# Column and row halves by turns in the chunk loop, the merge and the A products of a hybrid decoder block

## The chip, the cores and the metric

The kernel runs on one core of a Trainium2 chip. The metric is the device time of one execution in microseconds; the median of three runs is given. The engines are named as in the profile: PE (TensorE), with its weight loads as PEld, DVE (VectorE), ACT (ScalarE), POOL (GpSimd) and SP (SyncE, which issues the DMAs).

## The reference

A decoder block for a sequence of 2,048 tokens and a width of 1,024: RMS norm and modulation, one input projection, a convolution branch, an RWKV-7 branch with 16 heads of 64, gates, output projections, residual, final norm. The change touches the recurrence of the RWKV-7 branch:

```python
def step(state, inp):
    r_t, w_t, k_t, v_t, kk_t, b_t = inp
    sk = jnp.einsum('bhvk,bhk->bhv', state, kk_t)
    state = (state * w_t[:, :, None, :] - sk[..., None] * b_t[:, :, None, :]
             + v_t[..., None] * k_t[:, :, None, :])
    return state, jnp.einsum('bhvk,bhk->bhv', state, r_t)
```

## The kernel before

The sequence is cut into 4 blocks of 512 tokens, the 16 heads into 8 pairs of two heads (`hh` = 0, 1; each head has 64 of the 128 partitions), and two pairs (`q` = 0, 1) make a group: 4 groups a block, 16 in all. In a group the recurrence runs over 8 chunks of 64 tokens (`NCH` = 8, `CH` = 64): 128 chunks in all. Even and odd chunks (`e` = 0, 1) keep their rows in opposite halves of the partitions: `prow(e)` holds the rows of the solution, `vrow(e)` those of the values.

What a pair and a group do, in order:

- `pair` projects k, r and v (`mm3`, L195: an input of 128x512 against 128x128 weights in three products of high and low parts, recorded as passes with 256 or 512 columns), builds `KR` and `BK`, and the *A products* (L525): for each chunk and head one product of `BK` and `KR`, masked and evacuated to `As` by DVE (L527). So that one head's product can use all 128 partitions, ACT copies `BK` into `BKz`, whose other head's partitions are zero (L518). Four chunks of one head fill one PSUM bank (`aux`, two banks, which other steps of `pair` share).
- The inverse of a 64x64 triangle per chunk and head is made of its two 32x32 diagonal blocks, which POOL inverts (L594, L596; a DMA through DRAM before and behind it), and of the *merge*, which makes the off-diagonal block with 32x32 matmuls: L626 (lower), a DVE copy to `Qs` (L630), L635 (upper), a DVE copy into `As` (L640). Even and odd chunks are two runs of 16 matmuls each, first all of e = 0, then all of e = 1, in one PSUM bank (`late`).
- The *chunk loop* (L657 to L697). For each chunk: the state against `KR` (L668), the values against `As` (L673, 64 rows), DVE copies the sum to `X` (L676), the o matmuls of the chunk before (`olast`, L653) and their copy by ACT (L655), the *solution* (L682: `As` against `X`, 64 rows), DVE scales it into `uv` (L684), the state's update (L688) and four DVE operations that write the state `S` (L693). The next chunk begins with that state. Each of L653, L673 and L682 has four matmuls with 64 columns a chunk. Each chunk takes a new PSUM tile `xo` of two.

All f32 matmuls are issued as two passes, each with a weight load; the profile counts passes. The f32r ones of L195 are one pass each.

A scheduler orders the instructions of each engine by its own estimate of times and by priorities, so projections of the next pair, the convolution and the gates (`fill`) stand between the steps of the chunk loop in PE's queue, and DVE's 30 convolution taps a tile (L759) between the steps on DVE. Each engine works through its queue in order. `tc.issue_after(x)` keeps an instruction behind x in that order. L493 (`pair`) sums squares per chunk with 64-column matmuls whose output goes to the two partition halves by turns. Phase 2 (from L904 on: output projections, norm) is not touched.

Of the kernel before, what the change touches and what calls it, by code (L numbers as in the profile page):

```python
# [82 lines left out]
def hybrid_block(ctx: ExitStack, tc: tile.TileContext, x, vecs, convk, w2a2, final_g, ada, w_in, w_co, w_ro, w_o, crow, out,  # L83
# [193 lines left out]
    BKz = c1.tile([P, 2, NCH // 2, 4 * CH], F32, name="BKz")  # L277
    nc.gpsimd.memset(BKz[64:128, 0], 0.0)
    nc.gpsimd.memset(BKz[0:64, 1], 0.0)
    hones = bones.bitcast(F32)[:, 0::64]  # L280
    one = c1.tile([P, CH], F32, name="one")
# [164 lines left out]
    def pair(b, q_, pr, h, lora, uv, Asb, rn, res):  # L446
# [69 lines left out]
        for hh in range(2):  # L516
            hs = slice(64 * hh, 64 * hh + 64)
            nc.scalar.copy(BKz[hs, hh], BK[hs])  # L518
        for c4 in range(NCH // 4):
            for hh in range(2):  # L520
                pA = pa.tile([P, 2, 256], F32, name="aux", tag="aux")
                for c in range(4):
                    cc, e = (c4 * 4 + c) // 2, c % 2
                    es = slice(e * 128, e * 128 + 128)
                    nc.tensor.matmul(pA[:, c // 2, es], BKz[:, hh, cc, es], KR[:, cc, es],  # L525
                                     start=(c == 0), stop=(c == 3), skip_group_check=True)
                nc.vector.tensor_tensor(  # L527
                    out=Asb[:, hh, c4 * 4:c4 * 4 + 4, :].rearrange("p (a e) n -> p a (e n)", e=2),
                    in0=pA, in1=flat(maskA).unsqueeze(1).broadcast_to([P, 2, 256]), op=ALU.mult)
# [31 lines left out]
    def group(b, g, h, lora, fill):  # L561
        uv = l3.tile([P, NCH, 2, P], F32, name="uv", tag="uv", bufs=2)
        As = [l3.tile([P, 2, NCH, P], F32, name="As", tag="As", bufs=ASB) for _ in range(2)]
# [53 lines left out]
        pq = pl.tile([P, 2, 2, NCH // 2, 32], F32, name="late", tag="late")  # L617
        for e in range(2):
# [4 lines left out]
        for e in range(2):  # L623
            lo_, hi_ = quarters(e)
            for n, (q, hh, c) in enumerate(every):
                nc.tensor.matmul(pq[hi_, q, hh, c, :], As[q][lo_, hh, 2 * c + e, hi_], T11[lo_, q, hh, c, :],  # L626
                                 start=(n == 0), stop=(n == 15), skip_group_check=True)
        for e in range(2):
            lo_, hi_ = quarters(e)
            nc.vector.tensor_copy(Qs[hi_], pq[hi_])  # L630

        for e in range(2):
            lo_, hi_ = quarters(e)
            for n, (q, hh, c) in enumerate(every):
                nc.tensor.matmul(pq[lo_, q, hh, c, :], Qs[hi_, q, hh, c, :], As[q][hi_, hh, 2 * c + e, hi_],  # L635
                                 start=(n == 0), stop=(n == 15), skip_group_check=True)
        for e in range(2):
            lo_, hi_ = quarters(e)
            for q in range(2):
                nc.vector.tensor_copy(As[q][lo_, :, e::2, hi_], pq[lo_, q])  # L640
# [4 lines left out]
        prev = None  # L645

        def olast(c, xo):

            vr, rc = vrow(c % 2), rcol(c % 2)
            for q in range(2):  # L650
                for hh in range(2):
                    hs = slice(64 * hh, 64 * hh + 64)
                    nc.tensor.matmul(xo[vr, q, hs], As[q][:, hh, c, rc], uv[:, c, q, hs],  # L653
                                     start=False, stop=(q == 1 and hh == 1), skip_group_check=True)
            nc.scalar.copy(O[vr, c // 2], xo[vr, 0:2])  # L655

        for c in range(NCH):  # L657
            cc, e = c // 2, c % 2
            pr_, vr = prow(e), vrow(e)
# [467 lines left out]
```

## Time and profile before

| | |
|---|---|
| median of 3 runs | 3123.53 us (3115.43 to 3130.16) |
| the profiled execution | 3119.74 us, of which the span of the trace is 3118.0 us |
| granted clock of TensorE, mean | 0.984 |
| A products L525 | 1024 passes, 136.6 us busy |
| o L653, values L673, solution L682 | 1024 passes each; 87.3, 87.2 and 89.7 us busy |
| merge L626 and L635 | 1024 passes each; 36.0 and 33.9 us busy |
| projections L195 with 256 columns | 3 × 4608 passes, 958 us busy each |
| convolution taps L759 on DVE | 928, 698.0 us busy |
| DMA | 667.79 MB, mean 214 GB/s |

Passes are pipelined and overlap in the trace, so their busy times add up to more than PE's share of the span; what a pass costs is read from the distance between starts. A row of a group reads: line, engine, operation, output<-inputs, tile of the array, shape, count, then busy time and mean ns of one, then the engine's idle time before them and what ended it. A row of a timeline reads: start, duration, engine, line, operation and count of what was merged.

### The profile page before, as it was taken

How to read it: one execution, taken by the hardware profiler on the slowest of the kernel's cores; microseconds unless marked ns; L12 is line 12 of the kernel's file. 1: busy time of each engine (PE TensorE's matmuls, PEld its weight loads, DVE VectorE, ACT ScalarE, POOL GpSimd, SP SyncE). 2: the span in 40 equal slices, each digit the busy share in tenths (PEclk: the TensorE clock that was granted, in tenths of full speed). 3: DMA queues.
4: the chain of work that ended last, by engine and by line, in shares of the span. 5: the costliest groups of instructions: out<-in, count | busy, mean ns of one | idle time of the engine just before them, and what ended most of it. 6: DMA issues, size and time to landing. Idle time of an engine off the chain costs nothing. (4 is left out here: it accounts for less than half of the span.)

```text
span 3118.0 us, 64926 instructions
## 1 busy us (share of the span) xinstructions
PE 2980.5 (96%) x25648; PEld 2804.4 (90%) x25648; DVE 2138.2 (69%) x4282; ACT 1018.6 (33%) x1868; POOL 1142.4 (37%) x1708
## 2 busy tenths in 40 slices
PE   6799998999999999999999999999999999799998
PEld 6689998989999999999999999999999978678888
DVE  6676867686767676767676677767688535986633
ACT  4424343433233332323232414132332213342311
POOL 3354435433433325142424335316256013653100
PEclk9899999999999999999999999999999999899999
DMA  7665758573747476547565767646458657777665
GB/s 297 214 239 193 258 187 278 192 236 133 251 139 256 136 242 230 197 138 233 159 221 166 260 211 262 196 142 208 139 178 267 215 204 271 282 250 274 216 223 176
DMA packets 354849, 667.79 MB, mean 214 GB/s; under 512 B 134704, under 2 KB 153456, under 8 KB 354544
## 3 DMA queue, kind: packets, MB, share of 16 engines
q1 hardware_dynamic: 354544, 663.64, 63.2%
q8 instruction: 202, 3.31, 0.4%
q14 instruction: 103, 0.84, 0.1%
HBM read 483.07 MB, written 179.31 MB: 212 GB/s over the span
## 5 line engine op out<-in xcount | busy, mean ns | idle before, releaser
L195 PE MATMUL ps_main<-h_hi,w_hi 128*128 128x256 f32 x4608 | 958.1, 285 | 24.4 <-ACT w_hi L178 19.1
L195 PE MATMUL ps_main<-h_hi,w_lo 128*128 128x256 f32 x4608 | 958.6, 285 | 9.0 <-POOL w_lo L180 7.6
L195 PE MATMUL ps_main<-h_lo,w_hi 128*128 128x256 f32 x4608 | 958.1, 285 | 0.0
L195 PEld LDWEIGHTS ps_main<-h_hi,w_hi 128*128 128x128 f32 x4608 | 718.3, 189 | 35.9 <-ACT w_hi L178 20.2
L195 PEld LDWEIGHTS ps_main<-h_hi,w_lo 128*128 128x128 f32 x4608 | 716.7, 189 | 18.0 <-POOL w_lo L180 9.4
L195 PEld LDWEIGHTS ps_main<-h_lo,w_hi 128*128 128x128 f32 x4608 | 716.3, 189 | 7.3 <-issue 0.7
L759 DVE SCALAR_TENSOR_TENSOR acc<-u,ck,acc 128x512 f32<-128x512 f32 x928 | 698.0, 752 | 20.1
L594 POOL TENSOR_TENSOR itmp<-La,TT 128x126 f32<-128x126 f32 (+22 forms) x496 | 179.4, 362 | 147.5 <-DMA La<-dA 112.0
L693 DVE SCALAR_TENSOR_TENSOR S<-xo,pe,Se 64x64 f32<-64x64 f32 x512 | 144.9, 283 | 107.9 <-PE xo L688 98.6
L178 ACT CAST w_hi<-w_st 128x1024 fp32r<-128x1024 f32 x103 | 107.9, 1048 | 293.7 <-DMA w_st<-w_in_t 144.0
L596 POOL TENSOR_TENSOR TT<-TT,itmp 128x126 f32<-128x126 f32 (+22 forms) x496 | 190.0, 383 | 35.8
L663 ACT ACTIVATE Se<-S,pe 128x128 f32<-128x128 f32 x256 | 88.9, 394 | 228.7 <-DVE S L693 228.3
L180 POOL TENSOR_TENSOR w_lo<-w_st,w_hi 128x1024 fp32r<-128x1024 f32 x47 | 112.2, 2388 | 136.8 <-ACT w_hi L178 98.2
L548 POOL TENSOR_TENSOR vv<-rk,vv 128x512 f32<-128x512 f32 x32 | 43.5, 1359 | 295.7 <-ACT rk L547 295.7
L684 DVE TENSOR_TENSOR uv<-xo,rn 64x256 f32<-64x256 f32 x128 | 53.8, 421 | 131.8 <-PE xo L682 130.7
L525 PE MATMUL aux<-KR,BKz 128*128 128x128 f32 x1024 | 136.6, 278 | 2.6 <-DVE As L527 1.8
L180 DVE TENSOR_TENSOR w_lo<-w_st,w_hi 128x1024 fp32r<-128x1024 f32 x56 | 75.6, 1349 | 82.4 <-PE ps_main L195 51.3
L525 PEld LDWEIGHTS aux<-KR,BKz 128*128 128x128 f32 x1024 | 123.8, 191 | 5.0 <-DVE As L527 2.0
L527 DVE TENSOR_TENSOR As<-aux,maskA 128x512 f32<-128x512 f32 x128 | 86.9, 687 | 46.7 <-PE aux L525 46.1
L676 DVE COPY X<-xo 64x256 f32<-64x256 f32 x128 | 53.7, 420 | 91.6 <-PE xo L673 90.7
L655 ACT COPY uv<-xo 64x256 f32<-64x256 f32 x128 | 46.8, 366 | 186.2 <-PE xo L653 185.7
L668 PE MATMUL xo<-S,KR 128*128 128x128 f32 x512 | 95.7, 279 | 1.2 <-DVE S L693 1.1
(290 smaller groups left out, 5497.5 us busy)
## 6 DMA issues: line engine op xcount, KB each, us to landing
w_hi<-kh_in SPq DMA_DIRECT2D x219, 512.0 KB, 3.9
w_lo<-kl_in SPq DMA_DIRECT2D x219, 512.0 KB, 5.0
w_st<-w_in_t SPq DMA_DIRECT2D x73, 512.0 KB, 4.6
kh_in<-w_hi SPq DMA_DIRECT2D x71, 512.0 KB, 3.0
kl_in<-w_lo SPq DMA_DIRECT2D x71, 512.0 KB, 4.5
w_hi<-kh_ro SPq DMA_DIRECT2D x32, 512.0 KB, 4.3
w_lo<-kl_ro SPq DMA_DIRECT2D x32, 512.0 KB, 5.8
w_st<-w_co_t SPq DMA_DIRECT2D x32, 512.0 KB, 3.5
```

What stands on the lines that cost most here:

```text
L178: nc.scalar.copy(hi, st)
L180: lo_eng.tensor_tensor(out=lo, in0=st, in1=hi.bitcast(F32), op=ALU.subtract)
L195: nc.tensor.matmul(ps[:, qs], ww[:, k, :], aa[k][:, qs], start=(k == 0 and t == 0 and q == 0), stop=(k == KT - 1 and t == 2 and q == ms - ...
L525: nc.tensor.matmul(pA[:, c // 2, es], BKz[:, hh, cc, es], KR[:, cc, es], start=(c == 0), stop=(c == 3), skip_group_check=True)
L527: nc.vector.tensor_tensor(out=Asb[:, hh, c4 * 4:c4 * 4 + 4, :].rearrange("p (a e) n -> p a (e n)", e=2), in0=pA, in1=flat(maskA).unsqueeze ...
L594: nc.gpsimd.tensor_tensor(out=tmp[:, :ni, :nt], in0=La[:, j:j + 1, j + 1:].broadcast_to([P, ni, nt]), in1=TT[:, :ni, j:j + 1].broadcast_to ...
L596: nc.gpsimd.tensor_tensor(out=TT[:, :ni, j + 1:], in0=TT[:, :ni, j + 1:], in1=tmp[:, :ni, :nt], op=ALU.add)
L663: nc.scalar.mul(Se[:, q, :], Sg[:, q, :], R[q]["pe"][:, c:c + 1])
L668: nc.tensor.matmul(xo[:, q, :], R[q]["KR"][:, cc, es], Sg[:, q, :], start=(q == 0), stop=False, skip_group_check=True)
L684: nc.vector.tensor_tensor(out=uv[pr_, c].rearrange("p q (h n) -> p q h n", n=64), in0=xo[pr_, 0:2].rearrange("p q (h n) -> p q h n", n=64) ...
L693: nc.vector.scalar_tensor_tensor(out=Sg[hs, q, hs], in0=xo[hs, 2 + q, hs], scalar=R[q]["pe"][hs, c:c + 1], in1=Se[hs, q, hs], op0=ALU.mult ...
L759: nc.vector.scalar_tensor_tensor(out=acc if i + 1 < HALO else yj, in0=u[:, i:i + TB], scalar=ck[:, j, i:i + 1], in1=acc, op0=ALU.mult, op1 ...
```

## The change

- *A products*: `BKz`, its fills and the copies of L518 go. Each head's product uses its own 64 partitions (tile 64x128), and the matmuls of the two heads stand by turns in the code, each into a bank of its own, so a set of four chunks holds both `aux` banks.
- *Merge*: even and odd chunks by turns instead of one after the other, in two banks (`late` and an `aux`); each matmul is kept behind the first one of its burst. The order of the pairs is reversed, the DVE operations begin with e = 1.
- *Chunk loop*: the two `xo` tiles are taken once a group. The value part of a chunk is computed a chunk ahead: `xval(c + 1, n)` stands by turns with the solution's matmuls of chunk c, in the opposite column half and in the other bank. It now uses all 128 rows; for that `uv`'s solution rows are set to zero by POOL at a group's start. ACT copies the result into `Xz`, and DVE adds the state's part to it there (in place of the copy to `X`). The solution uses all 128 rows too (`Xz` is zero in the other half). The o matmuls of two chunks stand by turns in one burst (`o2`), behind the solution of every second chunk; ACT keeps the state's part of o in `OS`, and DVE adds the two.

The number of matmuls is the same.

```diff
@@ pair
-        for hh in range(2):
-            hs = slice(64 * hh, 64 * hh + 64)
-            nc.scalar.copy(BKz[hs, hh], BK[hs])
         for c4 in range(NCH // 4):
+            pA = [pa.tile([P, 2, 256], F32, name="aux", tag="aux") for _ in range(2)]
+            for c in range(4):
+                cc, e = (c4 * 4 + c) // 2, c % 2
+                es = slice(e * 128, e * 128 + 128)
+                for hh in range(2):
+                    hs = slice(64 * hh, 64 * hh + 64)
+                    nc.tensor.matmul(pA[hh][:, c // 2, es], BK[hs, cc, es], KR[hs, cc, es],
+                                     start=(c == 0), stop=(c == 3), skip_group_check=True)
             for hh in range(2):
-                pA = pa.tile([P, 2, 256], F32, name="aux", tag="aux")
-                for c in range(4):
...
-                    nc.tensor.matmul(pA[:, c // 2, es], BKz[:, hh, cc, es], KR[:, cc, es],
-                                     start=(c == 0), stop=(c == 3), skip_group_check=True)
@@ group
+        for e in range(2):
+            nc.gpsimd.memset(uv[prow(e), e::2], 0.0)
...
-        pq = pl.tile([P, 2, 2, NCH // 2, 32], F32, name="late", tag="late")
+        pq = [p_.tile([P, 2, 2, NCH // 2, 32], F32, name=n_, tag=n_) for p_, n_ in ((pl, "late"), (pa, "aux"))]
...
+        def turns(mul):
+            mm = []
+            for n, (q, hh, c) in enumerate(every[::-1]):
+                for e in range(2):
+                    with tc.issue_after(mm[-1].ins) if mm else nullcontext():
+                        mm_ = mul(e, q, hh, c, dict(start=(n == 0), stop=(n == 15), skip_group_check=True))
+                    mm = mm if n else mm + [mm_]
...
+        xo = [px.tile([P, 4, P], F32, name="xo", tag="xo") for _ in range(2)]
+        def xval(c, n):
+            q, hh, hs = every[3 - n]
+            nc.tensor.matmul(xo[c % 2][prow(c % 2), 2 + q, hs], As[q][:, hh, c, kcol(c % 2)], uv[:, c, q, hs],
+                             start=(n == 0), stop=(n == 3), skip_group_check=True)
+        def xcopy(c):
+            nc.scalar.copy(Xz[prow(c % 2), c % 2], xo[c % 2][prow(c % 2), 2:4])
+        def o2(cc):
+            for n, (q, hh, hs) in enumerate(every):
+                for e in range(2):
+                    nc.tensor.matmul(xo[1][vrow(e), q, hs], As[q][:, hh, 2 * cc + e, rcol(e)], uv[:, 2 * cc + e, q, hs],
+                                     start=(n == 0), stop=(n == 3), skip_group_check=True)
+            nc.vector.tensor_tensor(out=O[:, cc], in0=xo[1][:, 0:2], in1=OS[cc], op=ALU.add)
...
+            nc.vector.tensor_tensor(out=Xz[pr_, e], in0=b_[pr_, 0:2], in1=Xz[pr_, e], op=ALU.add)
+            nc.scalar.copy(OS[cc][vrow(e)], b_[vrow(e), 0:2])
+            for n, (q, hh, hs) in enumerate(every):
+                with tc.issue_after(mm.ins) if n else nullcontext():
+                    mm_ = nc.tensor.matmul(b_[pr_, q, hs], As[q][:, hh, c, kcol(e)], Xz[:, e, q, hs],
+                                           start=(n == 0), stop=(n == 3), skip_group_check=True)
+                mm = mm if n else mm_
+                if c + 1 < NCH:
+                    with tc.issue_after(mm.ins):
+                        xval(c + 1, n)
+            if c and e == 0:
+                with tc.issue_after(mm.ins):
+                    o2(cc - 1)
+            if c + 1 < NCH:
+                xcopy(c + 1)
```

More of the change, by code (lines that the diff above doesn't have):

```diff
@@ L687, in group @@
             for q in range(2):
[L688 removed]
+                nc.tensor.matmul(b_[:, 2 + q, :], R[q]["tk"][:, c, :], uv[:, c, q, :], start=False, stop=(q == 1),
                                  skip_group_check=True)
[L690 to L695 removed]
```

82 lines of the change are left out of this document (27 added, 55 removed).

## The prediction

> **What bounds the kernel now.** I read the page's engine table first, then a table of stages, then PE's groups and waits, and last PE's own timeline.
>
> ```profile
> PE 2980.5 (96%) x25648; PEld 2804.4 (90%) x25648; DVE 2138.2 (69%) x4282; ACT 1018.6 (33%) x1868; POOL 1142.4 (37%) x1708
> ```
>
> ```profile
> 800.00:1100.00 300.00, 297.91 (x2826) 287.07 (x2825) 206.86 (x448) 93.94 (x180) 105.76 (x194) 1.00 0.61 197
> ...
> 2000.00:2300.00 300.00, 300.00 (x2824) 287.81 (x2823) 206.69 (x440) 92.42 (x168) 114.16 (x196) 1.00 0.52 171
> ```
>
> In the stages that hold the chunk loops (columns: length, PE, weight loads, DVE, ACT, POOL, granted clock, DMA share, GB/s) PE is busy for 298 to 300 of 300 us at a granted clock of 1.00, DVE for 207. A busy PE could still hide waits, so the waits come next.
>
> ```profile
> PE xo L688 <- DVE uv L684: 3.1, 4, 1.2
> PE xo L682 <- DVE X L676: 2.9, 4, 1.2
> ```
>
> Of the three steps that PE waits for in each of 128 chunks, these two stopped it four times each, 1.2 us at most (columns: sum, times, longest). The recurrence from chunk to chunk is covered by projections (L195), so the time is the sum of what PE issues. What each burst costs is read off the starts of PE's rows.
>
> ```profile
> 1019.42 0.40 PE L195 MATMUL ps_main<-h_lo,w_hi 128*128 128x256 f32 x2
> ...
> 1020.84 0.40 PE L195 MATMUL ps_main<-h_lo,w_hi 128*128 128x256 f32 x2
> ```
>
> Six pairs of projection passes lie between these two starts: 1.42/6 = 0.237 us a pair. A row counts passes; an f32 matmul is two, so the x8 below is four matmuls.
>
> ```profile
> 1025.43 0.39 PE L195 MATMUL ps_main<-h_lo,w_hi 128*128 128x256 f32 x2
> 1025.75 0.68 PE L682 MATMUL xo<-X,As 64*64 64x64 f32 x8
> 1026.36 0.51 PE L195 MATMUL ps_main<-h_hi,w_lo 128*128 128x256 f32 x2
> 1026.70 0.40 PE L195 MATMUL ps_main<-h_hi,w_hi 128*128 128x256 f32 x2
> ```
>
> From 1025.43 to 1026.70 are 1.27 us; two pairs of projections take 0.47, so the solution burst costs PE 0.80. Of these, 0.61 lie between its start and the next; the other 0.20 is lost before and behind it, where the tile shape changes from 128*128 to 64*64 and back.
>
> ```profile
> 1008.70 0.40 PE L195 MATMUL ps_main<-h_lo,w_hi 128*128 128x256 f32 x2
> 1008.93 0.60 PE L668 MATMUL xo<-S,KR 128*128 128x128 f32 x4
> 1009.47 0.67 PE L673 MATMUL xo<-uv,As 64*64 64x64 f32 x8
> 1010.07 0.68 PE L653 MATMUL xo<-uv,As 128*64 128x64 f32 x8
> 1010.68 0.50 PE L195 MATMUL ps_main<-h_hi,w_lo 128*128 128x256 f32 x2
> 1011.02 0.40 PE L195 MATMUL ps_main<-h_hi,w_hi 128*128 128x256 f32 x2
> ```
>
> The other half of a chunk: 2.32 us less 0.47 for two pairs and 0.44 for L668 (four passes at the 0.111 worked out below) leave 1.41 for L673 and L653.
>
> **The change part by part.** *Chunk loop.* Before, a chunk has three small bursts: 1.41 + 0.80 = 2.21 us, times 128 chunks = 283 us. After, the value matmuls of the next chunk stand by turns with the solution's of this one. Both have 128 rows and 64 columns, in opposite column halves. The o matmuls of two chunks are a second burst by turns. Whether two halves run at once is shown by L493, which alternates column halves already:
>
> ```profile
> 1001.47 0.40 PE L195 MATMUL ps_main<-h_hi,w_hi 128*128 128x256 f32 x2
> 1001.80 0.68 PE L682 MATMUL xo<-X,As 64*64 64x64 f32 x8
> 1002.40 0.63 PE L493 MATMUL aux<-bones,sq 128*64 128x2 f32 x16
> 1002.97 0.51 PE L195 MATMUL ps_main<-h_lo,w_hi 128*128 128x256 f32 x2
> ```
>
> Sixteen passes with alternating halves take 0.57 us, eight with one half (L682) 0.60. Per pass L493 needs about (0.63 − 0.20)/15 = 0.029 us (its last one lasts 0.20 by its group on the page, 22.0 us over 512, of 200 ns), so one half alone 0.057. L493 streams two columns only, the new bursts 64, and no row shows two 64-column streams at once. One bound is therefore full overlap, the other none; I take overlap, as the 8-pass bursts with 64 columns and L493's slots agree in length, which makes the weight load, not the stream, the limit.
>
> [...]
>
> In the changed kernel's instruction order there are 64 bursts of eight matmuls by turns, 47 of these with eight o matmuls behind them (one more is split), 16 solutions without a partner (the last chunk of a group), 16 last o bursts and 16 first value bursts. At 0.57 + 0.20 = 0.77 alone, 0.46 (16 × 0.029) for the added o, and 0.80 for four matmuls without turns: 64 × 0.77 + 47 × 1.23 + 16 × 0.80 + 16 × 0.77 + 16 × 0.80 = 145 us. Saved: 138 us; with no overlap (0.46 more for 64 and for 16, 0.92 for 47) 80 less, 58.
>
> *Merge.*
>
> ```profile
> 976.77 0.39 PE L195 MATMUL ps_main<-h_hi,w_hi 128*128 128x256 f32 x2
> 977.09 2.11 PE L626 MATMUL late<-T,As 32*32 32x32 f32 x64
> 979.13 0.50 PE L195 MATMUL ps_main<-h_lo,w_hi 128*128 128x256 f32 x2
> 979.47 0.39 PE L195 MATMUL ps_main<-h_hi,w_lo 128*128 128x256 f32 x2
> ```
>
> 2.70 − 0.47 = 2.23 us a burst, 32 bursts (two a group): 71 us. A pass is (2.11 − 0.19)/63 = 0.0305. The two halves meet only in the middle of the burst now; two windows of 0.5 us, one before the middle and one over it, count the passes that touch them:
>
> ```profile
> 977.09 0.88 PE L626 MATMUL late<-T,As 32*32 32x32 f32 x22
> ...
> 977.68 0.85 PE L626 MATMUL late<-T,As 32*32 32x32 f32 x25
> ```
>
> Three more where the halves meet: they overlap there. By turns all the way, 64 passes take 32 slots: 0.98 us less, 31 us over 32 bursts. The order splits one matmul off 15 of the bursts, which costs an extra change of shape (between 0.20 and 0.80; I take 0.4): 6. Saved: 25 us.
>
> *A products.*
>
> ```profile
> 1018.06 0.40 PE L195 MATMUL ps_main<-h_hi,w_lo 128*128 128x256 f32 x2
> 1018.29 1.05 PE L525 MATMUL aux<-KR,BKz 128*128 128x128 f32 x8
> 1019.10 0.48 PE L195 MATMUL ps_main<-h_hi,w_hi 128*128 128x256 f32 x2
> ```
>
> To 1019.42 are 1.36 us, less 0.47: 0.89 for eight passes, 0.111 each, 114 us for 1024, and no change of shape. After, they are 64*128, in two row halves, so each burst leaves the shape of the projections: 0.80 less eight passes at 0.057 is 0.34 a round trip. The order has 73 such bursts alone and 20 beside other small ones (0.1 each): 27 us more. It alternates the halves at only 177 of 403 steps inside them; one pass overlapped at each gives back 177 × 0.111 = 20. Net 7 us dearer. Bounds: no overlap, 27 dearer; each burst only as long as its longer half (664 of 1024 passes by the order, 74 us), 13 cheaper.
>
> *Other engines.*
>
> ```profile
> L518 ACT COPY BKz<-BK 64x1024 f32<-64x1024 f32 x64 | 66.9, 1046 | 35.2 <-POOL BK L506 29.9 <-DVE BK L500 4.3 <-DVE ss L335 0.2
> L684 DVE TENSOR_TENSOR uv<-xo,rn 64x256 f32<-64x256 f32 x128 | 53.8, 421 | 131.8 <-PE xo L682 130.7
> L1055 DVE TENSOR_TENSOR xt<-pout,xt 128x256 f32<-128x256 f32 x64 | 24.2, 418 | 79.9 <-PE pout L1049 79.8
> L278 POOL MEMSET BKz<- x1: 950/950/950, 1.1 to 1.1; 64x1024 f32 x1
> ```
>
> ACT loses 64 copies (67 us) and gains 128 value copies like L655. DVE's X copy becomes an add of L684's shape; 64 o additions of L1055's shape come on top: 27 us. POOL gets 32 fills of 64x1024: 30 us. All lie under PE's 300 of 300 (DVE 207, POOL 114); uncovered, DVE's would cost 27, POOL's 30. No DMA is added.
>
> *Waits.* The order also tells how much PE work lies between the steps of a chunk. Less than 1.8 us (by the pass times above) stands between two dependent steps 33 times, 4 times before, mostly in a group's first chunks. PE's queue is in order, so all projections behind stand too. A step needs burst, DVE operation and next start; uncovered ones waited up to 1.2 us (rows of waits above). Those eight had a mean of 0.75, so I take 0.9 between it and the longest: 33 × 0.9 = 30 us; bounds 0 and 40.
>
> Sum: −138 − 25 + 7 + 30 = −126. The profiled execution took 3119.74 us, 1.74 over its span of 3118.0: 2992 + 2 = 2994 us. That execution lies 4 us under the median of the three runs, inside their spread of 15, so no correction is made.
>
> **The rivals.**
>
> *Column halves run one after the other.* [...] Against: L493. 2994 + 80 = 3074 us.
>
> *All overlaps, nothing waits.* For: the four waits of before and DVE at 69%; A bursts as long as their longer half. Against: the 33 short covers. −138 − 25 − 13 = −176: 2944 us.
>
> *PE queues at the two aux banks: slower.* An A product now fills both banks before either is read, and the merge holds one too.
>
> ```profile
> L527 DVE TENSOR_TENSOR As<-aux,maskA 128x512 f32<-128x512 f32 x128 | 86.9, 687 | 46.7 <-PE aux L525 46.1
> PE aux L525 <- DVE As L527: 1.8, 1, 1.8
> ```
>
> PE's next user of a bank stands behind two evacuations, 1.37 us, and what DVE has ahead of them; a group has four such places, 64 in all. Slower needs 126 + 16 us over 64, so it decides from 2.2 us a place. With two other DVE operations of 0.75 in front at each, 2.9 × 64 = 186: 3180 us. Against it: one such wait before, and projections stand between most of these bursts in the order.
>
> *The PE time saved comes back as waiting for DVE in the chunk loops.* In the late chunks of a group the order lays nearly as much DVE work as PE work between two chunks. Then nothing is gained: 3120 us. Against it: 207 of 300.
>
> **How the numbers follow.** Forecast 0.65, column halves in series 0.13, everything overlapping 0.10, no gain 0.05, aux banks 0.07. Half a per cent, 16 us, is about what a measurement of this kernel can tell from no change. Faster: 0.65 + 0.13 + 0.10 = 0.88; same 0.05; slower 0.07. The range goes from 2945 (second rival) to 3090, which takes in the first rival and A products without overlap; it leaves out about 0.15. The likeliest case by itself: −170 to −80, 2950 to 3040.
>
> **What would show it.** Right: in the timeline after, sixteen passes of solution and next values between projections cost about 0.77 us and thirty-two with o 1.23, a merge burst lasts about 1.1 us instead of 2.11, and PE stays near 298 of 300 in the group stages, which themselves are shorter. The step on the A products is right if a burst with unbroken halves goes on at 0.111 us a pass, and with alternating ones at half that. Wrong: sixteen passes near 1.1 us (first rival); waits of PE for DVE evacuations of A over 100 us in sum (third); PE's share in the group stages falling to 93% with its passes cheaper as worked out (fourth).

## The result and the profile after

The changed kernel takes 3176.9 us (median of four runs, 3174.86 to 3179.34) against 3123.05 us for the kernel before beside it: ratio 1.0179, 95% interval 1.0163 to 1.0195. It is slower by 54 us where 126 to 129 less were forecast. Its profiled execution took 3175.16 us with a span of 3173.0.

The first line is from the engine table of the page, the three others from the table of stages (columns as before the change: length, PE, weight loads, DVE, ACT, POOL, granted clock, DMA share, GB/s):

```profile
PE 2910.4 (92%) x25648; PEld 2719.8 (86%) x25648; DVE 2197.8 (69%) x4346; ACT 997.4 (31%) x1932; POOL 1181.1 (37%) x1739
```

```profile
800.00:1100.00 300.00, 282.10 (x2728) 268.42 (x2727) 210.36 (x438) 91.10 (x188) 104.50 (x179) 0.94 0.57 186
2000.00:2300.00 300.00, 290.10 (x2898) 278.85 (x2897) 216.82 (x432) 85.66 (x173) 116.31 (x201) 0.98 0.54 177
2300.00:2500.00 200.00, 164.18 (x1540) 153.58 (x1539) 167.95 (x322) 56.83 (x107) 101.75 (x177) 0.85 0.53 175
```

PE is busy for 70 us less (2980.5 before) in a span that is 55 us longer. In the stages that were 298 to 300 of 300 it now stands 10 to 18 us, and the granted clock, 1.00 there before, is 0.94 and 0.98; from 2300 to 2500 it stands 36 of 200 us at 0.85.

Two numbers per kernel carry what follows. *Idle* is span less PE's busy time: 137.5 us before, 262.6 after. The granted clock in these traces is either 1.00 or 0.50 (its mean is 0.984 before and 0.948 after), and *clock loss* is half of the time for which PE was busy at 0.50: 72.7 us at half clock before, so 36 lost; 243.7 us after, so 122 lost. This reckons that work takes twice as long at half clock. In the trace after, a projection pass with 256 columns started 0.213 us behind the one before it at half clock and 0.118 at full (medians, 1.8 times), one with 512 columns 0.427 and 0.227 (1.9 times), so the clock loss is an estimate somewhat too high: at 1.8 times it rises by 76 us instead of 86, and the work falls by 146 instead of 156. What is left of the busy time without the clock loss, the *work at full clock*, fell from 2944 to 2789 us. The balance: −156 of work, +125 of idle, +86 of clock loss, together +55. Reckoned so, the work fell by just what the bursts were forecast to save (−138 − 25 + 7 = −156).

Did the bursts become as cheap as worked out? PE's timeline of the changed kernel, a solution burst in a stage at full clock:

```profile
919.69 0.40 PE L195 MATMUL ps_main<-h_hi,w_hi 128*128 128x256 f32 x2
920.01 0.27 PE L699 MATMUL xo<-Xz,As 128*64 128x64 f32 x1
920.02 0.27 PE L664 MATMUL xo<-uv,As 128*64 128x64 f32 x1
...
920.47 0.22 PE L699 MATMUL xo<-Xz,As 128*64 128x64 f32 x1
920.48 0.22 PE L664 MATMUL xo<-uv,As 128*64 128x64 f32 x1
920.63 0.51 PE L195 MATMUL ps_main<-h_lo,w_hi 128*128 128x256 f32 x2
920.97 0.40 PE L195 MATMUL ps_main<-h_hi,w_lo 128*128 128x256 f32 x2
```

From 919.69 to 920.97 are 1.28 us, less two pairs (0.47): 0.81 for sixteen passes, 0.77 forecast. The two halves start 0.01 us apart, and the next two 0.05 to 0.06 behind (0.11 behind the first two). The median of 24 such bursts that stand between projections at full clock is 0.81, and that of 35 with the o matmuls behind them 1.28 (1.23 forecast). The merge likewise:

```profile
858.66 0.28 PE L195 MATMUL ps_main<-h_lo,w_hi 128*128 128x256 f32 x1
858.87 0.21 PE L636 MATMUL late<-T,As 32*32 32x32 f32 x1
858.88 0.21 PE L636 MATMUL aux<-T,As 32*32 32x32 f32 x1
...
859.88 0.19 PE L636 MATMUL aux<-T,As 32*32 32x32 f32 x1
860.00 0.50 PE L455 MATMUL aux<-lw,wl 128*128 128x512 f32 x1
```

64 passes from 858.87 to 859.88, and 860.00 − 858.66 less one pass (0.12) is 1.22 us a burst where 2.23 were. So the work was saved. What came instead stands in PE's waits (sum, times, longest):

```profile
PE xo L664 <- DVE As L651: 26.9, 10, 7.4
PE xo L699 <- ACT OS L694: 21.8, 14, 5.2
PE ps_main L195 <- ACT w_hi L178: 20.6, 6, 9.8
PE late L747 <- POOL uv L742: 18.6, 1, 18.6
...
PE xo L714 <- DVE uv L710: 16.3, 13, 4.4
PE xo L691 <- DVE S L717: 13.5, 9, 4.5
```

Over all rows of this view PE waits 84 us at `xo` (8 before) and 36 at `late` (6 before). By the engine that ended them, its waits grew from 70 to 137 us for VectorE, from 37 to 72 for ScalarE and from 9 to 30 for GpSimd; those for DMA stayed at 11.

### The profile page after: what moved, and what is told of

Read it like the earlier page. It is cut to its first block, busy times and chain, and to the rows that moved or that the text cites. A ratio compares the mean times of both kernels' runs of the same rounds, so it can differ in the third digit from the quotient of the medians.

```text
span 3173.0 us, 65210 instructions
## 1 busy us (share of the span) xinstructions
PE 2910.4 (92%) x25648; PEld 2719.8 (86%) x25648; DVE 2197.8 (69%) x4346; ACT 997.4 (31%) x1932; POOL 1181.1 (37%) x1739
## 4 chain that ended last, share of the span: by engine, by line
PE 51%; DVE 17%; DMA 12%; POOL 8%; issue 5%; SPq 3%; ACT 3%; POOLq 0%; DVEq 0%; ACTq 0%
PE ps_main L195 37%; DMA w_st<-w_in_t 4%; POOL TT L597 3%; POOL itmp L595 3%; PE aux L523 3%; DVE M L466 2%; DVE acc L782 2%; DMA La<-dA 1%; PE pout L1071 1%; PE pout L1070 1%; PE pout L1072 1%; PE xo L699 1%; DMA dT<-TT 1%; PE xo L714 1%; PE xo L691 1%
## 5 line engine op out<-in xcount | busy, mean ns | idle before, releaser
L195 PE MATMUL ps_main<-h_hi,w_hi 128*128 128x256 f32 x4608 | 972.0, 289 | 39.8 <-ACT w_hi L178 20.6
L195 PE MATMUL ps_main<-h_hi,w_lo 128*128 128x256 f32 x4608 | 973.1, 289 | 9.8 <-POOL w_lo L180 7.1
L195 PEld LDWEIGHTS ps_main<-h_hi,w_hi 128*128 128x128 f32 x4608 | 731.9, 193 | 50.5 <-ACT w_hi L178 21.7
L195 PEld LDWEIGHTS ps_main<-h_hi,w_lo 128*128 128x128 f32 x4608 | 730.6, 193 | 20.7 <-POOL w_lo L180 8.8
L195 PEld LDWEIGHTS ps_main<-h_lo,w_hi 128*128 128x128 f32 x4608 | 730.4, 193 | 6.5 <-issue 0.2
L523 PE MATMUL aux<-KR,BK 64*128 64x128 f32 x1024 | 123.4, 302 | 10.0 <-POOL BK L506 4.6
L523 PEld LDWEIGHTS aux<-KR,BK 64*128 64x128 f32 x1024 | 101.4, 199 | 25.6 <-POOL BK L506 6.4
L710 DVE TENSOR_TENSOR uv<-xo,rn 64x256 f32<-64x256 f32 x128 | 53.5, 418 | 100.1 <-PE xo L699 49.5
L664 PE MATMUL xo<-uv,As 128*64 128x64 f32 x1024 | 91.7, 236 | 26.9 <-DVE As L651 26.9
L691 PE MATMUL xo<-S,KR 128*128 128x128 f32 x512 | 102.9, 298 | 14.6 <-DVE S L717 13.5
L668 ACT COPY Xz<-xo 64x256 f32<-64x256 f32 x128 | 46.7, 365 | 214.4 <-DVE uv L676 113.2
```

The lines of the kernel that those rows point to most:

```text
L195: nc.tensor.matmul(ps[:, qs], ww[:, k, :], aa[k][:, qs], start=(k == 0 and t == 0 and q == 0), stop=(k == KT - 1 and t == 2 and q == ms - ...
L523: nc.tensor.matmul(pA[hh][:, c // 2, es], BK[hs, cc, es], KR[hs, cc, es], start=(c == 0), stop=(c == 3), skip_group_check=True)
L664: nc.tensor.matmul(xo[c % 2][prow(c % 2), 2 + q, hs], As[q][:, hh, c, kcol(c % 2)], uv[:, c, q, hs], start=(n == 0), stop=(n == 3), skip_g ...
L691: nc.tensor.matmul(b_[:, q, :], R[q]["KR"][:, cc, es], Sg[:, q, :], start=(q == 0), stop=False, skip_group_check=True)
```

## The experiments

The first eight runs compare parts of the change; what they and the later ones gave is put together in a table behind the last of them.

**One bank for the merge**, and **the state's part of o copied later**. The largest suspects by the waits: the merge's second bank, and the solution's wait for ACT's copy.

```diff
-        pq = [p_.tile([P, 2, 2, NCH // 2, 32], F32, name=n_, tag=n_) for p_, n_ in ((pl, "late"), (pa, "aux"))]
+        pq = [pl.tile([P, 2, 2, NCH // 2, 32], F32, name="late", tag="late")] * 2
```

> The changed kernel with both halves of the merge in the one bank late, as before the change, still by turns. Theory 1 (the merge's second bank is one of the two aux banks; while it is held, the scheduler lays little work between the first steps of a group's chunk loop, PE waits there and its clock is halved): PE's idle time falls from 263 to about 160 us, the granted clock rises from 0.948 to about 0.98, time 3000 to 3050 us. Theory 2 (the solution now waits for ACT's copy of o in every chunk) and theory 3 (the first value burst waits for the merge): nothing of theirs is touched, so 3160 to 3180 us.

```diff
-            nc.scalar.copy(OS[cc][vrow(e)], b_[vrow(e), 0:2])
             for n, (q, hh, hs) in enumerate(every):
...
+            nc.scalar.copy(OS[cc][vrow(e)], b_[vrow(e), 0:2])
             if c and e == 0:
```

> The changed kernel with ACT's copy of the state's part of o issued behind the solution burst, so that the solution waits for DVE's add alone. Theory 2: the 22 us of waits for that copy go, and with them the halved clock behind them: 3130 us or less. Theory 1: at most 20 us less than 3177, that is 3157 or more. Theory 3: the same as theory 1.

Measured: 3183.0 and 3193.0 us. Neither edit wins anything back; the second ends its own wait (the solution then waits 10.8 us for DVE's `Xz`, and no longer for `OS`), and the time goes up all the same.

**The merge of before** and **the chunk loop of before**, each in the changed kernel:

```diff
-        turns(lower)
+        for e in range(2):
+            lo_, hi_ = quarters(e)
+            for n, (q, hh, c) in enumerate(every):
+                nc.tensor.matmul(pq[hi_, q, hh, c, :], As[q][lo_, hh, 2 * c + e, hi_], T11[lo_, q, hh, c, :],
...
```

> The merge of before (two runs in one bank), with the new chunk loop and the new A products. Theory 1: the recovery of the one-bank run less the merge's 25 us of PE work: 3025 to 3075 us. Theory 2 and theory 3: the loss stays, 3180 to 3205 us.

```diff
-                with tc.issue_after(mm.ins) if n else nullcontext():
-                    mm_ = nc.tensor.matmul(b_[pr_, q, hs], As[q][:, hh, c, kcol(e)], Xz[:, e, q, hs],
...
+                    nc.tensor.matmul(xo[pr_, q, hs], As[q][pr_, hh, c, kcol(e)], X[pr_, q, hs],
...
```

> The chunk loop of before, with the new merge (two banks) and the new A products. By the terms of the prediction PE's work is 25 us less for the merge and 7 more for the A products: 3105 us if nothing waits. Theory 1 in its plain form (the bank alone is what hurts): 3150 us or more. Theories 2 and 3 put all of the loss into the new chunk loop: 3095 to 3115 us. If the bank hurts only together with the new loop, the same.

Measured: 3180.1 and 3200.0 us. With the new loop gone the kernel is slower still, so the loss isn't in the loop alone.

**A new order with the same work**, first try, and **less work for PE** in the kernel before:

```diff
-        for e in range(2):
+        for e in (1, 0):
...
-            for n, (q, hh, c) in enumerate(every):
+            for n, (q, hh, c) in enumerate(every[::-1]):
```

> The kernel before, with the same work: only the sequence in which the code emits the merge's operations differs (the DVE transposes begin with the odd chunks, the 16 matmuls of each run are emitted in reverse). Theory 4 (any edit makes the scheduler lay all queues anew, and a new order costs PE some 100 us of waits and halved clock that the order of before happens not to have): 3160 to 3200 us, granted clock near 0.95. Theory 5 (the new work itself, in queues of DVE, ACT and POOL that are late for a faster PE, makes the waits): no work is changed, 3110 to 3140 us, clock 0.98.

```diff
-        for t, (ww, aa) in enumerate(((whi, ahi), (whi, alo), (wlo, ahi))):
+        prods = ((whi, ahi), (whi, alo), (wlo, ahi))[:2 if skip[0] else 3]
+        for t, (ww, aa) in enumerate(prods):
```

> The kernel before, with the product of the low weights left out of the gate projections 3 and 4: 1024 passes of 0.118 us less, 121 us of PE work. If PE's work sets the time (the prediction's ground): 3000 to 3015 us. Theory 5: the other engines' queues take over, 3080 to 3125 us, with PE's idle time up by most of 121. Theory 4: 121 less, but a new order's 50 to 75 us on top, 3050 to 3080 us.

Measured: 3117.7 us, no difference, but this swap left 91% of PE's order as it was and so tests little. The other took 1024 projection passes away and gained 17 us of the 121 that they cost (ratio 0.9944, 0.993 to 0.9959). PE's line of its page:

```profile
PE 2903.0 (94%) x24624; PEld 2719.2 (88%) x24624; DVE 2173.2 (70%) x4282; ACT 1011.7 (33%) x1868; POOL 1148.0 (37%) x1708
```

In a span of 3101.7 that is 199 us idle, 61 more than before.

**The A products alone** and **the merge alone**, in the kernel before:

```diff
-                    nc.tensor.matmul(pA[:, c // 2, es], BKz[:, hh, cc, es], KR[:, cc, es],
+                    nc.tensor.matmul(pA[hh][:, c // 2, es], BK[hs, cc, es], KR[hs, cc, es],
```

> The new A products alone in the kernel before. By the prediction's term 7 us dearer, 3130 us (bounds 3110 and 3150). Theory 4: 3160 to 3200 us. Theory 6 (the pair of A products that takes both aux banks is what hurts, since all five slow kernels have it): 3170 to 3200 us, and the merge alone is not slower.

```diff
+        turns(lower)
...
+        turns(upper)
```

> The new merge alone in the kernel before. By the prediction's term 25 us less, 3098 us. Theory 4: 3140 to 3180 us. Theory 6: 3095 to 3110 us.

Measured: 3163.1 us (1.0133) and 3170.7 us (1.0158). The merge alone saves 26 us of work, as forecast, and is slower by 49 us. Every mix of the change's parts costs 41 to 72 us against the kernel before that ran beside it, whatever it does for PE's work, and so the next runs ask what an edit costs that changes no work.

**Two swaps that change no work**, and **the merge in two banks without turns**, in the kernel before, and one swap in the changed kernel:

```diff
-            for hh in range(2):
+            for hh in (1, 0):
                 pA = pa.tile([P, 2, 256], F32, name="aux", tag="aux")
```

> The kernel before with one swap in the program's text: the two column halves of every A product are issued as half 1, half 0 instead of half 0, half 1. Every pass, copy and transfer is the same work in the same shapes; but the scheduler lays the queues out anew (of TensorE's runs of equal instructions 58% stand in the same sequence as before; in the alone-standing merge 59%, in the changed kernel 42%). Theory 4 (what is lost in every one of these kernels is the order itself: the order of before fits and any new one costs TensorE waits and half clock): 3155 to 3180, ratio 1.010 to 1.018, TensorE's idle time 50 us or more above the 137 of before. Theory 5 (the order is neutral; TensorE's saved work turns into waits because the other queues are close behind): ratio within 0.997 to 1.003, idle time as before.

```diff
-            for q in range(2):
-                nc.tensor.matmul(xo[:, q, :], R[q]["KR"][:, cc, es], Sg[:, q, :], start=(q == 0), stop=False,
+            for q in (1, 0):
+                nc.tensor.matmul(xo[:, q, :], R[q]["KR"][:, cc, es], Sg[:, q, :], start=(q == 1), stop=False,
```

> The kernel before with another swap: in every chunk the product of KR with the state is issued for pair 1 first and then for pair 0. The same work in the same shapes; 55% of TensorE's runs of instructions keep their sequence. Theory 4: 3155 to 3180, as in the run before this one, though another place of the program was touched. Theory 5: ratio within 0.997 to 1.003. If one of the two swaps is slower and the other isn't, the order matters but not every new order costs.

```diff
-        pq = pl.tile([P, 2, 2, NCH // 2, 32], F32, name="late", tag="late")
+        pq = [p_.tile([P, 2, 2, NCH // 2, 32], F32, name=n_, tag=n_) for p_, n_ in ((pl, "late"), (pa, "aux"))]
```

> The kernel before with merge's halves in two banks (late and one aux) but in the order of before, first all of one half, then all of the other: the same passes, none overlapped. 49% of TensorE's runs keep their sequence. Theory 4: 3155 to 3190. Theory 5: within 0.997 to 1.003 (or up to 10 us more for the aux bank that merge now holds 16 times).

> The changed kernel with the swap of the second run (KR with the state, pair 1 before pair 0): the same work as the changed kernel, another order. Theory 4: the order is drawn anew, so the time may differ from the 3177 of the changed kernel by up to 1% either way, with TensorE's busy time at 2910 and the difference all in idle time and clock. Theory 5: within 0.3% of 3177, since the same waits come back whatever the order.

Measured: 3127.8 us (1.0009, 0.9996 to 1.0023), 3164.2 us (1.0131, 1.0102 to 1.016), 3183.6 us (1.0182, 1.0156 to 1.0209), and 3185.3 us for the changed kernel with the swap. PE's lines of the second and third:

```profile
PE 2996.5 (95%) x25648; PEld 2817.5 (89%) x25648; DVE 2171.6 (69%) x4282; ACT 1017.8 (32%) x1868; POOL 1147.0 (36%) x1708
```

```profile
PE 3022.3 (95%) x25648; PEld 2836.5 (89%) x25648; DVE 2164.7 (68%) x4282; ACT 1018.0 (32%) x1868; POOL 1144.0 (36%) x1708
```

The passes are the same 25648. Yet swapping two independent products costs 38 us and taking a second bank 58; the other swap costs 2 us, within its interval of none. So an edit that only draws a new order is worth from nothing to 1.3% here. The third run has a bank more as well; giving that bank back in the changed kernel won nothing, but that was a new order too, so the bank's own share of the 58 us is not shown. Theory 4 as first put, that every new order costs, fails by the halves' swap.

**The order of before, with work taken out afterwards.** From here on the instructions are changed after the scheduler has laid them out, so that each queue keeps its sequence and its waits. First by fewer streamed columns, in the chunk loop's small passes (64 to 32), then in the projections of the earlier run (256 to 16):

```diff
     with tile.TileContext(nc, schedule_with_timeline_sim=True) as tc:
         hybrid_block(tc, *args, out)
+    for f in nc.m.functions:
+        for blk in f.blocks:
+            for i, ins in enumerate(list(blk.instructions)):
+                if type(ins).__name__ == "InstMatmult" and tuple(ins.tile_size) in ((128, 64), (64, 64)):
...
+                        blk.instructions[i] = replace(ins, ins=[cut_(ins.ins[0]), ins.ins[1]], outs=[cut_(ins.outs[0])])
```

> The kernel before with the order of every queue and every wait kept as scheduled; only afterwards the small passes of the chunk loop (L673, L682, L653) are cut from 64 streamed columns to 32, so that half of each burst's result is left out. It takes from TensorE about what the changed kernel takes from it in the chunk loop (some 138 us of 283), without the new order. Theory 4 (the new order loses what the work saves): 2985 to 3020, TensorE's busy time near 2840 and its idle time below 180. Theory 5 (the other in-order queues, VectorE's first, are close behind TensorE, and what TensorE no longer works it waits): 3080 to 3115, busy time near 2850 and idle time above 220.

> The same way, with the work that an earlier run left out (the low-weight product of the third and fourth gate projections, 1024 passes of 256 columns): here the passes stay where they are in the order of before and are cut to 16 columns, so that nearly all of that product is left out; some 110 us less for TensorE. The earlier run, with a new order, gave back 17 us of 121. Theory 4: 3010 to 3040. Theory 5: as the earlier run, 3085 to 3112.

Measured: 3116.8 and 3132.4 us, and both miss their purpose, for the cut took next to nothing from PE. PE's timeline of the second:

```profile
1132.83 0.28 PE L195 MATMUL ps_gate<-h_hi,w_lo 128*128 128x16 f32 x2
1132.97 0.48 PE L195 MATMUL ps_gate<-h_hi,w_hi 128*128 128x256 f32 x2
1133.28 0.39 PE L195 MATMUL ps_gate<-h_lo,w_hi 128*128 128x256 f32 x2
1133.51 0.28 PE L195 MATMUL ps_gate<-h_hi,w_lo 128*128 128x16 f32 x2
```

Six passes take 0.68 us with two of them cut to 16 columns, and three pairs of 0.237, 0.71, without. The start behind a short pair comes after 0.14 us, but the one behind the pair that follows only after 0.31: what the short pass saves, the next one loses. The weight loads of the cut passes took as long as those of the passes beside them (162.6 us busy for 1024, 162.4 and 162.8 for the two others), and in the trace before a pass costs 0.111 us with 128 columns of weights (L525), 0.058 with 64 (L682) and 0.0305 with 32 (L626). That the load sets the cost is the author's reading of these numbers; no run changed the loads alone.

**The convolution cut short**, in the changed kernel and in the one before, each in its order: VectorE's 928 taps from 512 columns to 128.

```diff
+                if ins.outs and len(ins.ins) == 3 and getattr(ins.ins[2], "ap", ((0, 0),))[-1][1] == 512 and getattr(ins.outs[0], "memref", "").startswith("acc_"):
...
+                    blk.instructions[i] = replace(ins, ins=[cut_(a) for a in ins.ins], outs=[cut_(ins.outs[0])])
```

> The changed kernel with its order kept; afterwards the 928 steps of the convolution on VectorE (L782, 0.753 us each, 699 us in all) are cut from 512 columns to 128, so that three quarters of the convolution are left out: some 400 us less for VectorE, nothing less for TensorE. Theory 5: TensorE's waits go with what stands ahead of VectorE's short copies in its queue: 2960 to 3060, idle time from 263 to below 160 and the granted clock up. If the waits are the chunk's own chain (copy, burst, copy, in series) or the order of TensorE itself: above 3130.

> The kernel before with the same cut of the convolution's steps, as the control. Theory 5: TensorE waits little here (138 us idle, most of it in the first and last stages, where the convolution isn't), so 3080 to 3120; the gain is well below that of the changed kernel. If VectorE bounded both kernels alike: the same gain in both, over 80 us.

Measured: 3186.2 and 3118.8 us. DVE works 369 us less in the first (2197.8 to 1829.2), and PE's idle time stays at 262 us. The taps are not what PE waits for, and theory 5 in that form falls.

**Whole passes taken out**, the order of before kept, and **the chain's own copies cut** in the changed kernel:

```diff
+                if type(ins).__name__ == "InstMatmult" and tuple(ins.tile_size) in ((128, 64), (64, 64)) and ins.outs[0].ap[-1][1] == 64:
+                    if ins.sync_info is None:
+                        continue
+                keep.append(ins)
```

> The kernel before in its own order, from which 975 of the 1536 small products of the chunk loop (L673, L682, L653; each two passes with two weight loads) are taken out after the scheduling, namely those that neither wait nor release anything; their part of the result is left out. What stays keeps its place and its waits. Cutting the streamed columns, as in an earlier run, took nothing from TensorE, because the weight loads stayed; here they go too: 1950 passes of 58 ns, about 114 us. Theory 4 (the saved work would have paid in the order of before, and the new order loses it): 3005 to 3035, idle time below 170. Theory 5 (TensorE's saved work turns into waits in any order): 3080 to 3115, idle time above 200 and more half clock.

```diff
+                if ln in (668, 693, 710, 717) and type(ins).__name__ in ("InstTensorTensor", "InstTensorScalarPtr", "InstActivation", "InstTensorCopy"):
...
+                        return replace(a, ap=[list(a.ap[0]), [a.ap[-1][0], 8]])
```

> The changed kernel in its own order; afterwards the copies of the chunk's chain (L668 on ScalarE, L693, L710 and the four L717 on VectorE) are cut to 8 columns, so that most of each is left out. Every burst of TensorE stays, and each hop of the chain is shorter by some 0.1 to 0.2 us, some 0.8 us a chunk. Theory 7 (TensorE's waits at xo are the chain's own hops: the order leaves too little other work between two bursts of a chunk): the waits at xo fall from 84 us to below 45 and the time to 3090 to 3140. If the waits are what stands ahead in the queues of VectorE and ScalarE, or come from the order of TensorE's own work: above 3155, waits at xo above 65.

Measured: 3060.1 us (0.98, 0.9782 to 0.9817) and 3186.9 us (1.0208). PE's line and two of its waits in the first, three of its waits in the second:

```profile
PE 2884.1 (95%) x23698; PEld 2700.2 (88%) x23698; DVE 2138.0 (70%) x4282; ACT 1016.2 (33%) x1868; POOL 1142.2 (37%) x1708
```

```profile
PE xo L682 <- DVE X L676: 12.7, 10, 3.9
...
PE xo L688 <- DVE uv L684: 7.0, 6, 1.7
```

```profile
PE xo L664 <- DVE As L651: 27.0, 10, 7.4
PE xo L699 <- ACT OS L694: 26.0, 15, 5.4
...
PE xo L714 <- DVE uv L710: 10.3, 9, 4.2
```

In the order of before, about 114 us less work bring 63 us: between the two expectations (3005 to 3035, and 3080 to 3115), so more than half of the saving pays and 30 us come back as idle time, 11 as clock loss. In the changed kernel the chain's hops are not what the waits consist of: cut to 0.16 us from 0.42 (L693 and L710) and from 0.37 (L668), they leave 78 of the 84 us at `xo`.

All kernels in one table (us; the ratio is to the kernel before in the same series, 3122 to 3128 us; idle, clock loss and work of the profiled execution, as defined above):

| kernel | time | ratio | idle | clock loss | work at full clock |
|---|---|---|---|---|---|
| before | 3123 | 1 | 138 | 36 | 2944 |
| changed | 3177 | 1.018 | 263 | 122 | 2789 |
| merge in one bank | 3183 | 1.019 | 288 | 99 | 2787 |
| o's copy later | 3193 | 1.021 | 263 | 123 | 2794 |
| merge of before | 3180 | 1.018 | 257 | 105 | 2810 |
| loop of before | 3200 | 1.024 | 191 | 83 | 2922 |
| merge reversed (order 91% alike) | 3118 | 0.998 | 128 | 48 | 2941 |
| less PE work, new order | 3105 | 0.994 | 199 | 83 | 2820 |
| A products alone | 3163 | 1.013 | 138 | 73 | 2947 |
| merge alone | 3171 | 1.016 | 179 | 72 | 2918 |
| halves swapped, same work | 3128 | 1.001 | 130 | 47 | 2947 |
| states swapped, same work | 3164 | 1.013 | 161 | 52 | 2945 |
| two banks, same work | 3184 | 1.018 | 164 | 66 | 2956 |
| changed, states swapped | 3185 | 1.019 | 260 | 139 | 2782 |
| order held, 32 columns | 3117 | 0.998 | 143 | 39 | 2934 |
| order held, 16 columns | 3132 | 1.003 | 137 | 72 | 2927 |
| changed, short taps | 3186 | 1.020 | 262 | 136 | 2788 |
| before, short taps | 3119 | 0.999 | 130 | 46 | 2943 |
| order held, passes out | 3060 | 0.980 | 168 | 47 | 2837 |
| changed, short chain | 3187 | 1.021 | 262 | 125 | 2789 |

The last column bears out the reckoning and the sum of work part by part: kernels with the same work as before lie at 2941 to 2956, and the merge, the A products and the whole change at −26, +3 and −156 from 2944.

## Where the time went

What stands ahead of the short copies? VectorE's timeline of the changed kernel at the beginning of a group's chunk loop, and below it PE's at the same place:

```profile
1018.82 2.16 DVE L466 TENSOR_TENSOR_SCAN M<-one,M 128x64 f32<-128x64 f32 x8 [0.56 <-ACT M L458]
1021.01 0.76 DVE L651 COPY As<-late 32x256 f32<-32x256 f32 x2
...
1025.82 0.43 DVE L693 TENSOR_TENSOR Xz<-xo,Xz 64x256 f32<-64x256 f32 x1
1026.47 5.32 DVE L466 TENSOR_TENSOR_SCAN M<-one,M 128x64 f32<-128x64 f32 x8 [0.22 <-ACT M L458]
1031.82 0.43 DVE L710 TENSOR_TENSOR uv<-xo,rn 64x256 f32<-64x256 f32 x1
```

```profile
1021.82 0.69 PE L664 MATMUL xo<-uv,As 128*64 128x64 f32 x8 [1.66 <-DVE As L651]
...
1032.30 1.22 PE L714 MATMUL xo<-uv,tk 128*128 128x128 f32 x4 [4.45 <-DVE uv L710]
```

The scans of the *next* group's pair (L466) stand in VectorE's queue ahead of the merge's copy and again ahead of the first scaling; PE stands for 1.66 and 4.45 us behind them. In the kernel before the same place looks like this:

```profile
985.56 1.53 DVE L640 COPY As<-late 32x256 f32<-32x256 f32 x4 [0.90 <-PE late L635]
987.02 2.32 DVE L759 SCALAR_TENSOR_TENSOR acc<-u,ck,acc 128x512 f32<-128x512 f32 x3
989.99 0.43 DVE L684 TENSOR_TENSOR uv<-xo,rn 64x256 f32<-64x256 f32 x1 [0.65 <-PE xo L682]
```

There VectorE waits for PE, with taps in between that end in time; the first set of eight scans ended at 970.5, ahead of the merge, and the second began at 1011.0, in the midst of the chunk loop. Over the whole trace the two sets of a group start 6.5 to 15.1 us apart in the changed kernel (11.5 in the median), 8.6 to 87.4 before (24.7). The run with less work for PE in a new order has them 11.1 us apart in the median too; the two slower runs with the same work, 31.0 and 19.5.

In the run with the taps cut short the same wait is still there, behind the same scans:

```profile
1039.79 5.30 DVE L466 TENSOR_TENSOR_SCAN M<-one,M 128x64 f32<-128x64 f32 x8 [0.23 <-ACT M L458]
1045.13 0.43 DVE L710 TENSOR_TENSOR uv<-xo,rn 64x256 f32<-64x256 f32 x1
```

Counted over the trace from 250 to 2560 us, where two starts of PE are more than 0.5 us apart (less 0.2 for the pass): 34 places with 34 us before, 59 with 68 us with passes taken out, 124 with 184 us in the changed kernel. VectorE is busy in 150 of these 184 us: 33 of them with taps, 25 with the scans L466, 12 with L486, the rest in pieces of the pair's preparation, the inverse's and the chain's own operations. That is 82%, not far above the 72% for which it is busy in the whole stretch, so this count says less than the rows above. That these preparations are late because the scheduler, which orders by estimated times, now lays them beside the chunk loop's start is read from these rows; no run moved them alone, so it is argued and not shown.

The clock follows. The table of stages around the wait above:

```profile
1002.00:1019.00 17.00, 17.00 (x235) 16.60 (x235) 2.60 (x6) 6.58 (x14) 3.90 (x4) 1.00 0.66 215
1019.00:1022.00 3.00, 1.34 (x36) 0.87 (x30) 2.94 (x11) 1.29 (x3) 0.79 (x3) 1.00 0.92 259
1022.00:1040.00 18.00, 11.53 (x74) 9.69 (x74) 14.32 (x27) 8.52 (x18) 13.55 (x14) 0.53 0.48 156
```

PE is busy for 1.34 of 3 us, and then the granted clock is one half for 17 of the next 18 us. There are 18 such stretches in the trace before and 45 in the one after. They begin on a grid of 3.41 us, so the windows of this grid can be counted. In the trace after, 42 of the 45 stretches begin behind a window in which PE was busy for less than 54%; no window with less than 48% was followed by full clock. No stretch gave way to full clock behind a window with PE busy for less than 85%. Of the windows in which PE was busy for 54 to 85%, 47 of 50 at full clock were followed by full clock, and all 14 at half clock by half clock; with PE busy for 85% or more, 44 of 58 at half clock were followed by full clock. A stretch, once begun, thus went on behind windows that seldom began one.

Idle time isn't all of it. In the run with the A products alone a window of the grid in which PE was busy throughout was followed by half clock:

```profile
1184.00:1187.40 3.40, 3.40 (x76) 3.16 (x74) 1.50 (x6) 0.00 (x0) 1.18 (x1) 1.00 0.77 245
1187.40:1190.80 3.40, 3.40 (x18) 3.35 (x16) 3.28 (x5) 1.78 (x3) 1.35 (x2) 0.50 0.51 145
```

The first holds a merge burst (64 passes with 32x32 tiles) and eight passes of A products with 64x128 tiles; two more windows of that run are like it. Why the clock fell behind them is not shown.

## Why the prediction was wrong

- *Cheaper bursts, −138 and −25*: right, and so is overlap of two 64-column streams, the step for which no row stood. 0.81 us for 0.77 by turns, 1.22 for 2.23 in the merge (1.25 forecast). Work at full clock, reckoned as above, fell by 156 us, as forecast. The two halves started 0.01 us apart, and sixteen passes cost 0.81 us where the first rival's mark was 1.1, so the first rival falls.
- *A products, 7 dearer*: the work of that part alone is 2947 against 2944, so right within what the table can tell.
- *Waits, +30 (bounds 0 and 40)*: this step failed. Idle time rose by 125 us. The sum counted only covers inside the chain that became short, with 0.9 us each, and of VectorE, ScalarE and GpSimd it asked only whether their work fits under PE's. Inside the chain the count was about right and the price was not: the rows L699, L714, L691 and L674 have 37 waits where 33 were counted, but 56 us, 1.5 each. Another 27 us are the chunk loop's first burst behind the merge's copy (L651), and the rest lies outside the chain (`late` +31, `aux` and the projections), where the queues of the other engines had been laid anew.
- *The clock*: a term that the sum lacked. The granted clock was taken to stay at 0.984; it fell to 0.948, which by the reckoning above cost 86 us more of PE's busy time, and 42 of the 45 stretches at half clock began behind a window of 3.41 us in which PE stood for 46% or more.
- *The premise behind all of it*, that the time is the sum of what PE issues since the recurrence is covered: it holds for the order of before, and there by little more than half (63 of 114 us). It doesn't hold across orders: with no work changed the time goes up by 2, 38 and 58 us (the last with a bank more). The prediction used the new instruction order to count bursts and covers on PE, and didn't ask what the same new order does to the other queues.
- *The rivals*: waits of PE for DVE's evacuation of A products were 2.4 us in sum, so the third rival falls as a mechanism, though the time came out on its side. The mark of the fourth (PE's share falling to 93% with passes as cheap as worked out) is near what came, 282 and 290 of 300 and 164 of 200; but it put the waits into the late chunks of a group, behind VectorE's whole load, and ended at no gain. Cutting that load by 369 us changed nothing, and clock loss and new waits went past zero by 54 us. The second rival, that nothing waits, falls by the 125 us of idle time.

What stays open, first, is how much of the loss is the new order's. The slower orders with the same work added 24 and 27 us of idle time and 15 and 30 of clock loss, the changed kernel 125 and 86. The held order with 108 us less work added 30 and 11. Scaled to 156 us of work, these and the larger of the two slower orders come to an estimate of some 115 of the 211 us; no run shows the rest. The nearest to it is the run with less work for PE in a new order: 124 us less, 61 of idle time and 47 of clock loss more. Open too is whether the changed kernel in an order as good as that of before would be faster. Seven kernels with its loop, three of them with the same queues, took 3177 to 3193 us, none below before; that is no proof that no such order exists. Nor is it known why the A products alone, and the order held with 16 columns, lose some 36 us more of clock with no more idle time; windows like the one above are too few to explain it.

## What to carry to other kernels

Where a scheduler lays out the queues, an edit has two prices, that of its work and that of a new order, and the second can be the larger: measure it with edits that change no work, more than one of them (here 0 to 1.3%). Before taking work from a busy engine, take it out of the finished order once: that tells what the saving could bring at best. And price a wait of PE with what the clock adds to it: here 125 us of waits came with 86 us of clock.

## What the runs showed of the hardware

- Two column halves with 64 streamed columns ran at once, both on all 128 rows (tiles 128*64): starts 0.01 us apart, then 0.05 to 0.06 to the next pair (0.11 behind the first), 0.81 us for sixteen passes.
- Cutting streamed columns while the weight loads stayed saved next to nothing: 64 to 32 columns changed the busy time of the solution's 1024 passes from 89.7 to 85.6 us, and 256 to 16 in two of six passes the distance from 0.71 to 0.68 us.
- The granted clock changed only between 1.00 and 0.50, on a grid of 3.41 us. In the trace after, half clock came behind windows with PE busy for less than 54% (42 of 45), and full clock came back only behind windows with at least 85%; with the A products alone, a window with PE busy for 3.40 of 3.40 us, with merge passes and A products in it, was also followed by half clock. At half clock a projection pass with 256 columns took 0.213 us from start to start, at full clock 0.118.
- Eight scans of one shape took 2.16 us at one place and 5.32 us at another in the same group; POOL was busy for 0.79 of 3 us at the first and for 13.55 of 18 around the second. Whether POOL is the reason wasn't tried.
